# Norm of x in halves of the tokens, the first half scaled by a diagonal matrix in its transpose

## The chip, the cores and the metric

The kernel runs on one core of one Trainium2 chip. The metric is the device time of one execution in microseconds (us), smaller is better. Before the change three runs gave 636.5 us in the median, 636.15 at the lowest and 637.94 at the highest.

## The reference

One decoder layer for 512 tokens of width 1024, in float32:

```
h = RMSNorm(x); proj = h @ w_in            # 8 column groups of attention, RWKV-7 and memory queries
x = x + concat(diff_attention, rwkv7, memory_attention) @ w_out
x = x + hierarchical_moe(RMSNorm(x))       # 16 experts, top-2 inside one of 4 groups
```

Only the first two steps matter here: `h = x * rsqrt(mean(x*x) + eps) * gain`, row by row, and the first projection, whose 256 columns are the inputs of RWKV's small low-rank branches ("lor").

## The kernel before

TensorE multiplies with h as the transposed operand, so x (four tiles `f` of 128 tokens by 1024) has to be normed, transposed and split. Each float32 value is kept as a high part (float32r) and the rest (low part); a product is three matmuls: high by high, high by low, low by high. Weights come through `WeightStream`: a 512 KB chunk lands in `raw`, ScalarE writes its high part `whi` (L96), VectorE its low part `wlo` (L97).

The start is staged like this. For each of the four token tiles `row_scale` (L268) squares and sums on VectorE (L272), GpSimd makes the inverse root (L273, L274), ScalarE multiplies the tile by it (L279; the fourth tile on VectorE, L277). Then TensorE transposes the tile's eight 128-column blocks (L301) into eight PSUM banks, bank k holding block k of all 512 tokens. When all four tiles are in, `split_cols` takes each bank of 512 columns to `hm_h` (ScalarE, L283) and `hm_l` (VectorE, L284). `cols_unit` (L349) is the first projection unit: for each k, for two 128-column groups j, three matmuls of 512 columns (L243, L244, L245, reached through `mm3`), 48 in all, into two PSUM banks; each chunk of weights covers four k. After it ScalarE and VectorE write `lor`, and the next units (k, r, v) follow on TensorE without a break.

Every engine runs its own queue in order. The order within a queue comes from a scheduler that estimates times and follows priorities; the start had no hand-written order. Tiles are reused when their last reader is done, and a reader of a PSUM tile waits for all matmuls into that tile that stand ahead of it in the program.

Of the kernel before, what the change touches and what calls it, by code (L numbers as in the profile page):

```python
# [14 lines left out]
AF = mybir.ActivationFunctionType  # L15
# [32 lines left out]
def VEC(t):  # L48
    return t == 3
# [71 lines left out]
class Weave:  # L121
    """Emits the steps of several streams in the order of their estimated times."""

# [27 lines left out]
def hybrid_layer_kernel(ctx, tc, x, mem, positions, cols, w_in, w_kv, w_out, wa2, g2, ffn, wr, br,  # L151
# [44 lines left out]

# [1 line left out]
    A.preload_act_table_set("sigmoid_and_others")  # L198
    xs = [bR("f1", [P, 2, D]), bR("f2", [P, 2, D])]
    xt = [xs[t // 2][:, t % 2, :] for t in range(NT)]  # L200
    for t in range(NT):
        (nc.sync, nc.scalar)[t % 2].dma_start(xt[t], x[t * P:(t + 1) * P, :])
    col = const.tile([P, N_COLS], F32, name="col")
    nc.scalar.dma_start(col, cols)
    ident = const.tile([P, P], F32, name="ident")
# [61 lines left out]

    def row_scale(src, vec=False):  # L268
        ss = wk.tile([P, 1], F32, name="ssx", bufs=4)
        r = wk.tile([P, 1], F32, name="rsx", bufs=4)  # L270
        scr = b4("aw0", [P, D])
        V.tensor_tensor_reduce(scr, src, src, 1.0, 0.0, op0=ALU.mult, op1=ALU.add, accum_out=ss)  # L272
        G.tensor_scalar(r, ss, 1.0 / D, RMS_EPS, op0=ALU.mult, op1=ALU.add)  # L273
        rooted = G.tensor_tensor(r, r, mhalf, op=ALU.pow)  # L274
        if vec:
            for b in range(2):
                V.tensor_scalar(src[:, b * 512:(b + 1) * 512], src[:, b * 512:(b + 1) * 512], r, None, op0=ALU.mult)  # L277
        else:
            A.activation(src, src, AF.Copy, scale=r)  # L279
        return rooted  # L280
# [4 lines left out]

# [1 line left out]
    banks = [pp() for _ in range(4)] + [pt() for _ in range(2)] + [pc() for _ in range(2)]  # L287
    held = [ws.pair.pop() for _ in range(3)]
    ws.pump()
    for t in range(2):  # L290
        nc.sync.dma_start(m_sb[:, t, :], mem[t * P:(t + 1) * P, :])
# [5 lines left out]
    nc.sync.dma_start(posc, positions.rearrange("o (t p) -> p (o t)", p=P))  # L297
    for t in range(NT):
        rooted = row_scale(xt[t], VEC(t))
        for k in range(KC):  # L300
            T.transpose(banks[k][:, t * P:(t + 1) * P], xt[t][:, k * P:(k + 1) * P], ident)  # L301
    for k in range(KC):
        got_h = split_cols(banks[k], col[:, C_AN + k:C_AN + k + 1], h_hi[:, k, :], h_lo[:, k, :])
        if k == KH:
            ws.pair.extend(reversed(held))
            with tc.issue_after(got_h[0].ins), tc.issue_after(got_h[1].ins):
                ws.pump()

# [18 lines left out]

# [1 line left out]
    r_t = bR("r_t", [P, 2, S])  # L329
# [18 lines left out]

    def cols_unit(dst, mc, flag):  # L349
        ps = [pp() for _ in range(2)]  # L350
        for kh in range(2):
# [13 lines left out]
        flags.add(flag)  # L365
        return None
# [91 lines left out]
    def projections():  # L458
        yield from cols_unit(lor, 6, "lor")
        yield from cols_unit(k_t, 2, "k")  # L460
# [17 lines left out]

# [1 line left out]
    lw = b4("prod", [P, 512])  # L480
# [36 lines left out]
    def rwkv():  # L517
# [85 lines left out]

# [1 line left out]
        for ci in range(4):  # L605
# [60 lines left out]

# [1 line left out]
        V.memset(rs[:, 0:1024:33], 1.0)  # L668
# [91 lines left out]

# [1 line left out]
        y_sb = bR("r_t", [P, NT, 256])  # L762
# [38 lines left out]

# [1 line left out]
    lp = const.tile([P, 2], F32, name="lp")  # L803
# [173 lines left out]

# [1 line left out]
    def out_part(ps, t, i, w, ks, k0, k1, lead=0):  # L979
# [28 lines left out]

# [1 line left out]
    late = ctx.enter_context(tc.tile_pool(name="late", bufs=1, reuse_waits="tile"))  # L1010
# [181 lines left out]

# [1 line left out]
    gslot = rc.tile([P, NE], F32, name="gslot")  # L1194
# [153 lines left out]

# [1 line left out]
    pk = pl(32)  # L1350
# [74 lines left out]
```

## Time and profile before

| | us |
|---|---|
| median of 3 runs | 636.5 |
| span of the profiled execution | 635.0 |
| around that span, in the median run (636.5 less 635.0) | 1.5 |
| TensorE (PE) busy in the span | 605.9 |
| first transpose on PE | 9.72 |
| PE's last long wait of the start ends | 19.49 |

No time of its own is listed for the profiled execution beyond its span. PE, ACT, DVE, POOL and SP are TensorE, ScalarE, VectorE, GpSimd and SyncE; PEld is TensorE's weight load. In a timeline row the first number is the start in us from the start of the span, the second how long the row's instructions took together, `x4` how many there are, and the bracket how long the engine sat idle before it and what released it. Matmuls overlap, so what one costs is read from the distance of starts, not from its own length.

### The profile page before, as it was taken

The page shows a single profiled execution, that of the slowest core. Times are in us where ns is not written, and L with a number is a line of the kernel's source. Part 1 is how long each engine was busy: PE and PEld are TensorE (multiplying, and loading weights), DVE is VectorE, ACT ScalarE, POOL GpSimd, SP SyncE. Part 2 cuts the span into 40 slices and gives each one's busy share as a digit, 9 for nine tenths or more (in the row PEclk, how much of TensorE's full clock was granted, in tenths as well). Part 3 has the DMA queues.
Part 4 walks back from the last instruction along what each step waited for, and adds up shares of the span by engine and source line. Part 5 has one row for each costly group of instructions (what it writes and reads, how often), then busy time and mean ns, then how long its engine had stood idle before and what let it go on. Part 6 is the DMA issues. An engine that isn't in the chain of part 4 may idle for free.

```text
span 635.0 us, 10856 instructions
## 1 busy us (share of the span) xinstructions
PE 605.9 (95%) x3970; PEld 486.2 (77%) x3970; DVE 500.9 (79%) x893; ACT 413.0 (65%) x622; POOL 124.1 (20%) x129
## 2 busy tenths in 40 slices
PE   3899999999999998999999999999999999999992
PEld 3777899999998887769997677777776777777771
DVE  5754988699846698646468999999999999988991
ACT  3667433544457774655246778888888888888880
POOL 6701010344400123304001011110011111320001
PEclk9999999999999999999999999999999999999997
DMA  8523244222332033659698999999999999799913
GB/s 304 167 67 101 66 128 122 78 91 67 102 83 69 1 134 123 243 176 354 237 338 284 358 341 366 382 356 357 362 356 359 361 371 370 251 369 375 336 26 54
DMA packets 77501, 144.17 MB, mean 227 GB/s; under 512 B 12832, under 2 KB 30496, under 8 KB 77440
## 3 DMA queue, kind: packets, MB, share of 16 engines
q1 hardware_dynamic: 69200, 126.07, 56.1%
q0 software_dynamic: 3760, 13.24, 8.9%
q10 hardware_dynamic: 4480, 4.09, 2.0%
q8 instruction: 33, 0.54, 0.3%
q14 instruction: 28, 0.23, 0.1%
HBM read 131.72 MB, written 11.67 MB: 226 GB/s over the span
## 4 chain that ended last, share of the span: by engine, by line
PE 90%; DVE 4%; ACT 2%; DMA 2%; POOL 1%; issue 1%; POOLq 0%; ACTq 0%
PE pp L243 17%; PE pp L245 17%; PE pp L244 17%; PE py L244 4%; PE py L245 4%; PE py L243 4%; PE pp L985 3%; PE pp L986 2%; PE pp L987 2%; PE pp L1267 1%; PE pt L909 1%; PE pc L609 1%; PE py L1123 1%; PE pt L934 1%; PE pl L1090 1%; PE pp L1289 1%
## 5 line engine op out<-in xcount | busy, mean ns | idle before, releaser
L245 PE MATMUL pp<-whi,xl 128*96 128x512 f32 x264 | 104.0, 395 | 0.0
L244 PE MATMUL pp<-wlo,xh 128*96 128x512 f32 x264 | 103.8, 394 | 0.0
L243 PE MATMUL pp<-whi,xh 128*96 128x512 f32 x264 | 101.2, 394 | 0.8 <-ACT xh L1254 0.8
L97 DVE TENSOR_TENSOR wlo<-raw,whi 128x1024 fp32r<-128x1024 f32 x42 | 52.0, 1244 | 19.9 <-ACT whi L96 16.1
L1315 POOL DMA_INDIRECT out<-ye,sidx x16 | 23.2, 1452 | 226.1 <-DVE gidx L1217 105.8
L96 ACT ACTIVATE whi<-raw 128x1024 fp32r<-128x1024 f32 x42 | 44.1, 1058 | 33.0 <-PE pp L245 17.9
L243 PE MATMUL pp<-whi,hm_h 128*128 128x256 f32 x224 | 63.7, 285 | 0.0
L245 PE MATMUL pp<-whi,hm_l 128*128 128x256 f32 x224 | 62.8, 280 | 0.0
L244 PE MATMUL pp<-wlo,hm_h 128*128 128x256 f32 x224 | 62.7, 280 | 0.0
L243 PEld LDWEIGHTS pp<-whi,xh 128*96 128x96 f32 x264 | 42.5, 161 | 19.6 <-ACT xh L1254 1.3
L245 PEld LDWEIGHTS pp<-whi,xl 128*96 128x96 f32 x264 | 42.6, 161 | 18.4
L244 PEld LDWEIGHTS pp<-wlo,xh 128*96 128x96 f32 x264 | 42.5, 161 | 18.2
L244 PE MATMUL py<-wlo,hh 128*96 128x512 f32 x120 | 47.9, 399 | 0.0
L245 PE MATMUL py<-whi,hl 128*96 128x512 f32 x120 | 47.1, 392 | 0.0
L243 PE MATMUL py<-whi,hh 128*96 128x512 f32 x120 | 47.0, 392 | 0.0
L97 DVE TENSOR_TENSOR wlo<-u,whi 128x1024 fp32r<-128x1024 f32 x34 | 41.3, 1238 | 6.6 <-ACT whi L96 6.5
L97 DVE TENSOR_TENSOR wlo<-lraw,whi 128x1024 fp32r<-128x1024 f32 x36 | 42.6, 1217 | 2.8 <-ACT whi L96 2.7
L243 PEld LDWEIGHTS pp<-whi,hm_h 128*128 128x128 f32 x224 | 42.1, 188 | 1.5 <-issue 1.1
L244 PEld LDWEIGHTS pp<-wlo,hm_h 128*128 128x128 f32 x224 | 42.1, 188 | 0.9 <-issue 0.5
L245 PEld LDWEIGHTS pp<-whi,hm_l 128*128 128x128 f32 x224 | 42.1, 188 | 0.3
L96 ACT ACTIVATE whi<-lraw 128x1024 fp32r<-128x1024 f32 x36 | 37.1, 1058 | 5.1 <-PE pp L245 3.6
L96 ACT ACTIVATE whi<-u 128x1024 fp32r<-128x1024 f32 x34 | 35.1, 1055 | 4.6 <-PE pp L245 2.2
(397 smaller groups left out, 1555.3 us busy)
## 6 DMA issues: line engine op xcount, KB each, us to landing
raw<-in_w_in SPq DMA_DIRECT2D x22, 512.0 KB, 3.6
u<-in_wd SPq DMA_DIRECT2D x12, 512.0 KB, 8.0
lraw<-in_wg SPq DMA_DIRECT2D x12, 512.0 KB, 11.3
lraw<-in_wu SPq DMA_DIRECT2D x12, 512.0 KB, 8.7
lraw<-in_wd SPq DMA_DIRECT2D x12, 512.0 KB, 12.4
f<-in_wg SPq DMA_DIRECT2D x11, 512.0 KB, 7.2
u<-in_wu SPq DMA_DIRECT2D x11, 512.0 KB, 12.0
eraw<-in_wd SPq DMA_DIRECT2D x10, 512.0 KB, 13.5
```

Source lines behind the costliest of these rows:

```text
L96: nc.scalar.activation(hi, slot, AF.Copy)
L97: nc.vector.tensor_sub(lo, slot, hi.bitcast(F32))
L243: T.matmul(ps, ah, bh, start=first, stop=False)
L244: T.matmul(ps, ah, bl, start=False, stop=False)
L245: T.matmul(ps, al, bh, start=False, stop=last)
L609: T.matmul(ps[:, h * P:(h + 1) * P], bk[sr(q), ci, h], u1[sr(q), q, ci, h], start=True, stop=True)
L909: T.matmul(po[:, 0:P], aws[i % 2][:, kb * P:(kb + 1) * P], qk["v"][:, kb, h * P:(h + 1) * P], start=kb == 0, stop=kb == qb)
L934: T.matmul(po[rows, :], mv[:, mb, h * 64:(h + 1) * 64], aws[mb][:, 0:512], start=mb == 0, stop=mb == 1)
L985: T.matmul(o, ah, hi[:, k % 4, :], start=k == k0 and i == lead, stop=False, skip_group_check=True)
L986: T.matmul(o, ah, lo[:, k % 4, :], start=False, stop=False, skip_group_check=True)
L987: T.matmul(o, al, hi[:, k % 4, :], start=False, stop=k == k1, skip_group_check=True)
L1315: G.indirect_dma_start(out, bass.IndirectOffsetOnAxis(ap=si, axis=0), ye, None, compute_op=ALU.add)
```

## The change

The four tiles are taken as two halves of 256 tokens. In the first half the tiles are not scaled: `diag[t]` is the identity times the inverse roots, and a true float32 matmul of the tile with `diag[t]` transposes and scales at once (L314 of the new file). The squares of tiles 1 and 3 move to ScalarE (L274). The second half is scaled as before, in half tiles on ScalarE and VectorE (L349, L350), and transposed with the identity (L316). Splits are 256 columns wide (L284, L285) and two blocks k share one bank. The first projection unit is written out in the same place as 96 matmuls of 256 columns (`half_products`, L329 to L331) into the same two banks. ScalarE, VectorE and TensorE get the order of this block as it is written. Tiles 2 and 3 of x are loaded on ScalarE's DMA queue behind `col`.

```diff
-        scr = b4("aw0", [P, D])
-        V.tensor_tensor_reduce(scr, src, src, 1.0, 0.0, op0=ALU.mult, op1=ALU.add, accum_out=ss)
+        if vec:
+            V.tensor_tensor_reduce(b4("aw0", [P, D]), src, src, 1.0, 0.0, op0=ALU.mult, op1=ALU.add, accum_out=ss)
+        else:
+            A.activation(b4("aw1", [P, D]), src, AF.Square, accum_out=ss)
         G.tensor_scalar(r, ss, 1.0 / D, RMS_EPS, op0=ALU.mult, op1=ALU.add)
-        rooted = G.tensor_tensor(r, r, mhalf, op=ALU.pow)
...
+        return r, G.tensor_tensor(r, r, mhalf, op=ALU.pow)
+
+    def row_scale(src):
+        r, rooted = row_root(src)
+        A.activation(src, src, AF.Copy, scale=r)
...
+    def half_turn(hf, k, banks):
+        o = banks[k % 6][:, k // 6 * 256:k // 6 * 256 + 256]
+        for t in range(2):
+            src, dst = xt[2 * hf + t][:, k * P:(k + 1) * P], o[:, t * P:(t + 1) * P]
+            if hf == 0:
+                T.matmul(dst, src, diag[t], start=True, stop=True)
+            else:
+                T.transpose(dst, src, ident)
+
+    def half_split(hf, k, banks):
+        tk = slice(hf * 256, hf * 256 + 256)
+        o = banks[k % 6][:, k // 6 * 256:k // 6 * 256 + 256]
+        return split_cols(o, col[:, C_AN + k:C_AN + k + 1], h_hi[:, k, tk], h_lo[:, k, tk])
+
+    def half_products(hf, ks):
+        tk = slice(hf * 256, hf * 256 + 256)
+        for k in ks:
+            hi, lo = first_w[k // 4]
+            for j in range(2):
+                o, wh, wl = first_ps[j][:, tk], hi[:, k % 4, j * P:(j + 1) * P], lo[:, k % 4, j * P:(j + 1) * P]
+                T.matmul(o, wh, h_hi[:, k, tk], start=hf == 0 and k == 0, stop=False, skip_group_check=True)
+                T.matmul(o, wh, h_lo[:, k, tk], start=False, stop=False, skip_group_check=True)
+                T.matmul(o, wl, h_hi[:, k, tk], start=False, stop=k == KC - 1, skip_group_check=True)
+
+    with tc.manual_schedule(engines={mybir.EngineType.Activation, mybir.EngineType.DVE, mybir.EngineType.PE}):
+        roots = [row_root(xt[0]), row_root(xt[1], False)]
+        for t in range(2):
+            V.tensor_scalar(diag[t], ident, roots[t][0], None, op0=ALU.mult)
+        roots.append(row_root(xt[2]))
+        banks = [pt(), pt(), pc(), pc(), pp(), pp()]
         for k in range(KC):
-            T.transpose(banks[k][:, t * P:(t + 1) * P], xt[t][:, k * P:(k + 1) * P], ident)
-    for k in range(KC):
-        got_h = split_cols(banks[k], col[:, C_AN + k:C_AN + k + 1], h_hi[:, k, :], h_lo[:, k, :])
-        if k == KH:
-            ws.pair.extend(reversed(held))
-            with tc.issue_after(got_h[0].ins), tc.issue_after(got_h[1].ins):
-                ws.pump()
+            half_turn(0, k, banks)
+        weights()
+        for k in range(4):
+            half_split(0, k, banks)
+        weights()
+        roots.append(row_root(xt[3], False))
+        for k in range(4, KC):
+            half_split(0, k, banks)
+        for i in (2, 3):
+            A.activation(xt[i][:, 0:512], xt[i][:, 0:512], AF.Copy, scale=roots[i][0])
+            V.tensor_scalar(xt[i][:, 512:D], xt[i][:, 512:D], roots[i][0], None, op0=ALU.mult)
+        half_products(0, range(4))
+        banks = [pt(), pt(), pc(), pc(), pp(), pp()]
+        for k in range(4):
+            half_turn(1, k, banks)
+        half_products(0, range(4, KC))
+        for k in range(4, KC):
+            half_turn(1, k, banks)
+        for k in range(KC):
+            got_h = half_split(1, k, banks)
+        half_products(1, range(KC))
```

ScalarE's queue at the start, before (f tiles of x, whi high parts of weights, hm_h high parts of h, pp/pt/pc PSUM banks):

```order
L279 ACTIVATE f_96<-f_96,rsx 128x1024 x2
L279 ACTIVATE f_97<-f_97,rsx 128x1024
L96 ACTIVATE whi_80<-raw_79 128x1024
L283 ACTIVATE hm_h<-pp,col 128x512
L96 ACTIVATE whi_83<-raw_82 128x1024
L283 ACTIVATE hm_h<-pp,col 128x512 x3
L283 ACTIVATE hm_h<-pt,col 128x512 x2
L283 ACTIVATE hm_h<-pc,col 128x512 x2
```

Scaling of the tiles comes first there, and the splits are whole banks of 512 columns.

The same queue in the changed kernel (aw takes the squares that nobody reads, ssx their sum):

```order
L274 ACTIVATE aw_146,ssx<-f_96 128x1024
L96 ACTIVATE whi_80<-raw_79 128x1024
L284 ACTIVATE hm_h<-pt,col 128x256 x2
L284 ACTIVATE hm_h<-pc,col 128x256 x2
L96 ACTIVATE whi_83<-raw_82 128x1024
L274 ACTIVATE aw_196,ssx<-f_97 128x1024
L284 ACTIVATE hm_h<-pp,col 128x256 x2
L284 ACTIVATE hm_h<-pt,col 128x256 x2
L349 ACTIVATE f_97<-f_97,rsx 128x512 x2
L284 ACTIVATE hm_h<-pt,col 128x256 x2
L284 ACTIVATE hm_h<-pc,col 128x256 x2
```

The scaling of the tiles stood first and now, for the second half (L349), stands behind the first half's eight splits, two weight chunks and a square.

TensorE's queue before, from its last transposes to the first products:

```order
L301 MATMUL pp<-ident,f_97 128x128 x4
L301 MATMUL pt<-ident,f_97 128x128 x2
L301 MATMUL pc<-ident,f_97 128x128 x2
L243 MATMUL pp<-hm_h,whi_80 128x512
L244 MATMUL pp<-hm_l,whi_80 128x512
L245 MATMUL pp<-hm_h,wlo_81 128x512
```

All 32 transposes stand ahead of the first product there.

TensorE's queue in the changed kernel: the last diagonal products, the first products of the first half, and the place where the second half's transposes begin (qmT is the diagonal matrix):

```order
L314 MATMUL pt<-qmT_132,f_96 128x128
L314 MATMUL pt<-qmT_133,f_96 128x128
L329 MATMUL pp<-hm_h,whi_80 128x256
L330 MATMUL pp<-hm_l,whi_80 128x256
...
L331 MATMUL pp<-hm_h,wlo_81 128x256
L316 MATMUL pt<-ident,f_97 128x128 x4
L316 MATMUL pc<-ident,f_97 128x128 x4
L329 MATMUL pp<-hm_h,whi_83 128x256
```

Transposes of the second half now stand between the products of the first half's blocks 0 to 3 and those of its blocks 4 to 7, and the queue is worked off in this order.

## Rows read from the trace of the kernel before

**Rows 1.** The page's first lines: the span, and each engine's busy time.

```profile
span 635.0 us, 10856 instructions
PE 605.9 (95%) x3970; PEld 486.2 (77%) x3970; DVE 500.9 (79%) x893; ACT 413.0 (65%) x622; POOL 124.1 (20%) x129
```

**Rows 2.** Waits of PE: who for whom, us in total, times, longest.

```profile
PE pp L301 <- ACT f L279: 10.3, 2, 9.7
PE pp L243 <- DVE hm_l L284: 1.6, 2, 0.8
```

**Rows 3.** Timeline of PE, from its first transpose to the second unit.

```profile
9.72 1.11 PE L301 MATMUL pp<-ident,f 128*128 128x128 f32 x4 [9.72 <-ACT f L279]
...
14.07 1.06 PE L301 MATMUL pp<-ident,f 128*128 128x128 f32 x4
...
15.35 0.39 PE L301 MATMUL pc<-ident,f 128*128 128x128 f32 x2
15.57 0.60 PE L301 MATMUL pp<-ident,f 128*128 128x128 f32 x4
...
17.41 0.50 PE L243 MATMUL pp<-hm_h,whi 128*128 128x512 f32 x1 [0.80 <-DVE hm_l L284]
...
20.53 0.39 PE L245 MATMUL pp<-hm_h,wlo 128*128 128x512 f32 x1
...
34.27 0.38 PE L439 MATMUL pt<-ident,kT 128*128 128x128 f32 x2
```

**Rows 4.** Timeline of the start: squares on DVE, inverse roots on POOL.

```profile
5.28 1.23 DVE L272 CUSTOM_DVE_ANT_0 aw<-f 128x1024 f32<-128x1024 f32 x1 [3.66 <-DMA f<-in_x]
...
6.54 1.22 DVE L272 CUSTOM_DVE_ANT_0 aw<-f 128x1024 f32<-128x1024 f32 x1
6.61 1.21 POOL L273 TENSOR_SCALAR rsx<-ssx 128x1 f32<-128x1 f32 x1 [3.76 <-DVE ssx L272]
...
7.90 0.58 POOL L274 TENSOR_TENSOR rsx<-rsx,mhalf 128x1 f32<-128x1 f32 x1
...
11.16 0.19 POOL L273 TENSOR_SCALAR rsx<-ssx 128x1 f32<-128x1 f32 x1
```

**Rows 5.** Timeline of PE: float32 products of 128 columns, then products of 256.

```profile
85.88 1.49 PE L609 MATMUL pc<-u,f 64*128 64x128 f32 x14
87.30 0.39 PE L244 MATMUL pp<-wlo,hm_h 128*128 128x256 f32 x1
87.52 0.28 PE L245 MATMUL pp<-whi,hm_l 128*128 128x256 f32 x1
...
90.93 0.28 PE L245 MATMUL pp<-whi,hm_l 128*128 128x256 f32 x1
```

**Rows 6.** ACT and DVE: timeline rows, and an accumulator read from the groups.

```profile
21.41 2.05 ACT L96 ACTIVATE whi<-raw 128x1024 fp32r<-128x1024 f32 x2
34.07 0.63 ACT L524 ACTIVATE ths<-lor 64x512 f32<-64x512 f32 x1
44.54 0.47 ACT L283 ACTIVATE v_da<-pt,col 128x256 fp32r<-128x256 f32 x1
44.91 0.71 ACT L553 ACTIVATE f<-k_t,col 128x512 f32<-128x512 f32 x1
...
46.03 0.48 DVE L284 SCALAR_TENSOR_TENSOR qT<-pt,col,v_da 128x256 fp32r<-128x256 f32 x1 [0.29 <-ACT v_da L283]
...
L858 ACT ACTIVATION_READ_ACCUMULATOR f<-f,mx 128x1 f32 x20 | 3.8, 191 | 0.0
```

**Rows 7.** Timeline of PE at 245 to 251: three waits.

```profile
245.23 0.68 PE L779 MATMUL pc<-f,f 128*64 128x64 f32 x8 [0.80 <-DVE f L775]
...
248.67 0.68 PE L784 MATMUL pc<-f,u 64*64 64x64 f32 x8 [0.44 <-DVE f L781]
...
250.81 0.56 PE L985 MATMUL pp<-whi,hm_h 128*128 128x256 f32 x1 [0.43 <-ACT pown L879]
```

**Rows 8.** Windows of PE: stretch, length, busy (count), granted clock, DMA share, GB/s.

```profile
251.00:254.00 3.00, 3.00 (x15) 0.50 0.83 298
```

More of the change, by code (lines that the diff above doesn't have):

```diff
@@ L200, in hybrid_layer_kernel @@
     xt = [xs[t // 2][:, t % 2, :] for t in range(NT)]
-    for t in range(NT):
-        (nc.sync, nc.scalar)[t % 2].dma_start(xt[t], x[t * P:(t + 1) * P, :])
     col = const.tile([P, N_COLS], F32, name="col")
+    nc.sync.dma_start(xt[0], x[0:P, :])
+    nc.scalar.dma_start(xt[1], x[P:2 * P, :])
     nc.scalar.dma_start(col, cols)
@@ L266, in hybrid_layer_kernel, with row_root @@
     m_lo = bR("qT", [P, KC, M], F32R)
-    def row_scale(src, vec=False):
+    def row_root(src, vec=True):
         ss = wk.tile([P, 1], F32, name="ssx", bufs=4)
         r = wk.tile([P, 1], F32, name="rsx", bufs=4)
-        scr = b4("aw0", [P, D])
-        V.tensor_tensor_reduce(scr, src, src, 1.0, 0.0, op0=ALU.mult, op1=ALU.add, accum_out=ss)
+        if vec:
+            V.tensor_tensor_reduce(b4("aw0", [P, D]), src, src, 1.0, 0.0, op0=ALU.mult, op1=ALU.add, accum_out=ss)
+        else:
+            A.activation(b4("aw1", [P, D]), src, AF.Square, accum_out=ss)
         G.tensor_scalar(r, ss, 1.0 / D, RMS_EPS, op0=ALU.mult, op1=ALU.add)
-        rooted = G.tensor_tensor(r, r, mhalf, op=ALU.pow)
[L275 to L279, printed above, removed]
+        return r, G.tensor_tensor(r, r, mhalf, op=ALU.pow)
+    def row_scale(src):
+        r, rooted = row_root(src)
+        A.activation(src, src, AF.Copy, scale=r)
         return rooted
@@ L284, in split_cols @@
         return first, V.scalar_tensor_tensor(lo, ps, g, hi.bitcast(F32), op0=ALU.mult, op1=ALU.subtract)
-    banks = [pp() for _ in range(4)] + [pt() for _ in range(2)] + [pc() for _ in range(2)]
-    held = [ws.pair.pop() for _ in range(3)]
+    held = [ws.pair.pop() for _ in range(4)]
     ws.pump()
+    for t in (2, 3):
+        nc.scalar.dma_start(xt[t], x[t * P:(t + 1) * P, :])
     for t in range(2):
@@ L297, in hybrid_layer_kernel @@
     nc.sync.dma_start(posc, positions.rearrange("o (t p) -> p (o t)", p=P))
-    for t in range(NT):
-        rooted = row_scale(xt[t], VEC(t))
-        for k in range(KC):
-            T.transpose(banks[k][:, t * P:(t + 1) * P], xt[t][:, k * P:(k + 1) * P], ident)
-    for k in range(KC):
-        got_h = split_cols(banks[k], col[:, C_AN + k:C_AN + k + 1], h_hi[:, k, :], h_lo[:, k, :])
-        if k == KH:
-            ws.pair.extend(reversed(held))
-            with tc.issue_after(got_h[0].ins), tc.issue_after(got_h[1].ins):
-                ws.pump()
+    diag = [b4(f"qmT{t}", [P, P]) for t in range(2)]
@@ new lines, in hybrid_layer_kernel, with weights @@
+    first_ps = [pp() for _ in range(2)]
+    first_w = []
+    def weights():
+        ws.pair.append(held.pop())
+        ws.pump()
+        first_w.append(ws.use())
+    def half_turn(hf, k, banks):
[6 more added lines that the diff above has]
+                T.transpose(dst, src, ident)
@@ L309, in later @@
+    rooted = roots[3][1]
+    ws.pair.extend(reversed(held))
+    with tc.issue_after(got_h[0].ins), tc.issue_after(got_h[1].ins):
+        ws.cool()
     def later():
@@ L347, in hybrid_layer_kernel, with cols_unit @@
     mv = b4("mv", [P, 2, 256])
-    def cols_unit(dst, mc, flag):
-        ps = [pp() for _ in range(2)]
-        for kh in range(2):
+    def cols_unit(dst, mc, flag, ps=None):
+        done_ = ps is not None
+        ps = ps or [pp() for _ in range(2)]
+        for kh in range(0 if done_ else 2):
             hi, lo = ws.use()
@@ L458, in projections @@
     def projections():
-        yield from cols_unit(lor, 6, "lor")
+        yield from cols_unit(lor, 6, "lor", first_ps)
         yield from cols_unit(k_t, 2, "k")
```

## The prediction

> **What bounds the kernel now.** I read the page first: PE is busy for 605.9 of 635.0 us, DVE and ACT far less [rows 1]. A kernel like that ends when PE ends, so a change at the start is worth what it does to the moment from which PE runs without a break. Next the waits of PE: the largest by far, 10.3 us, is for ACT's scaling of the x tiles, 9.7 of it before the first transpose [rows 2]. Then PE's timeline of the start [rows 3]. PE begins at 9.72. The transposes start 0.21 us apart at first (six from 14.07 to 15.35) and 0.11 apart from 15.35 on (two by 15.57): PE's clock is at the lower of its two levels (1.2 GHz) until about 5.6 us after its first work, then at the higher (2.4 GHz). The products start at 17.41 and run without a gap from 20.53. From there 60 products of 512 columns start before the row at 34.27, 0.229 us each. The row at 20.53 is the ninth of the first unit's 48, so the remaining 40 end at 20.53 + 40 x 0.229 = 29.7. That moment, the end of the first projection unit on PE, is what I compare; behind it PE goes on in both kernels with the same work.
>
> **The start of PE.** What is removed: ACT's scaling in front of the first transposes, and the wait of the first inverse root behind the second square. Before, the first square began at 5.28 and the second at 6.54 [rows 4], so both tiles had landed by then. POOL's first small step took 1.21 us while DVE squared, but 0.19 at 11.16 with DVE almost idle [rows 4]. Now DVE has nothing to do behind the first square, so I count 0.19 and then 0.58 for the power [rows 4]: the first root at about 7.5. The second tile is squared on ACT from about 5.8: 1.03 us (half of the pair of 2.05) and an accumulator read of 0.19 [rows 6], 7.0; its two POOL steps follow the first root and end at about 8.3. With some 0.3 us for the diagonal on DVE PE runs steadily from 8.65, 1.1 us earlier than before.
>
> **The diagonal products.** They take the place of 16 transposes. A true float32 product of 128 columns goes to PE as two instructions: 14 instructions, seven products, took 85.88 to 87.30, 0.203 us for each product at the higher clock level, against 0.11 for a transpose [rows 5, 3]; so 0.43 at the lower level. All at the lower level they end at 8.65 + 16 x 0.43 = 15.5, all at the higher at 8.65 + 16 x 0.203 = 11.9. Nothing in the rows says when the clock rises here, so I take the 5.6 us of before: at 14.25, after 13 products, and the last three take 0.6, end 14.85. The earlier start is eaten by the doubled price. On this one step the Trainium skill, "TensorE: Matmul & The Clock Gate", section Terms, speaks against the change more strongly: it says the transpose mode is four times faster for float32 than an ordinary pass. The rows show twice. What the four would make of the time is a rival below.
>
> **The queue of ACT.** This is the step I give most weight. A reader of a PSUM tile waits for all matmuls into it that stand ahead, and block 6 shares the bank of block 0, block 7 that of block 1. So the first split can begin only behind the 14th of the 16 products and the second behind the last, at about 14.95; the halves don't overlap with the slow products. From there ACT works off its queue in order: seven more splits of 256 columns at 0.37 (44.54 to 44.91) = 2.6; a weight chunk, 1.03; the square of the fourth tile, 1.03 + 0.19; two half tiles scaled, for which a copy of 512 columns stands, 0.63 each, 1.26 [rows 6]. Sum 6.1: the second half's tiles are scaled at 21.05. PE in the meantime has only the 24 products of blocks 0 to 3. Products of 256 columns start 0.114 apart (30 steps from 87.52 to 90.93 [rows 5]), 2.7 us behind the first low part at 14.5 + 0.47 + 0.48 = 15.45 [rows 6], so it is through at 18.1. Then it stands before the second half's transposes for some 2.9 us, and 24 products whose operands have long been ready stand behind them in the queue. Nothing covers this wait: DVE, POOL and the loads all have slack there, and ACT's queue is what PE waits for.
>
> **The rest of the unit.** From 21.05: 8 transposes at 0.11 = 0.9, 24 products = 2.75, 8 transposes = 0.9, end at 25.6. Again no split of the second half can begin before the last blocks are transposed, so a second, short stop follows: one split on ACT and one on DVE, 0.47 + 0.48 + 0.1 for the hand-overs [rows 6] = 1.05 (before it was much the same: two such stops, 1.6 in sum [rows 2]). From 26.6 the remaining 47 products take 5.35: 31.95. The products themselves cost the same as before, 96 x 0.114 = 10.9 against 48 x 0.229 = 11.0.
>
> **The sum.** 31.95 - 29.7 = +2.3 us. It is made against the execution with the span of 635.0; the median of the runs is 636.5, 1.5 of it outside the span, which the change does not touch: 636.5 + 2.3 = **638.8 us**, 0.36% slower. With the bounds of the diagonal products (11.9 and 15.5) the unit ends between 29.0 and 32.6: -0.7 to +2.9, 635.8 to 639.4. Its own range, if the split pitch or the copies are off by a tenth too: 637.6 to 639.8. What else moves I cost at nothing. The zero fill and masks on POOL come some 6 us later, since POOL's queue waits for the fourth tile's sum; they are wanted by later units. Loads of x tiles 2 and 3 are queued behind a 26 KB load and not behind other x tiles, and are needed at 9 and 17 us. The second unit's weight splits follow the last splits on ACT and DVE and would be there at about 31: if they are late by some tenths, PE waits that long once.
>
> **Rivals.**
> 1. *The clock falls in the new gap.* At 245 to 251 PE waited 0.80, 0.44 and 0.43 us among small matmuls, and behind it the granted clock was 0.50 for the whole of 251 to 254 [rows 7, 8]. So much waiting was enough there, and 2.9 us in one piece is more. Against it: at the start PE also waited, 1.6 us in two pieces among products of 512 columns [rows 2], and kept its 0.229 afterwards. A fall as long as that one, 3.0 us at half the clock, costs up to 1.5, less if part of it lies in the gap: 638.8 + 1.5 = 640.3.
> 2. *The queue of ACT is not the bound, since the clock rises early.* If most of the diagonal products run at the higher level, everything behind them slides forward: 635.8 at best, 637 with half of them. For it: PE's work is denser from the start than before. Against it: the 5.6 us of before, also of dense work but for 0.6 us.
> 3. *Not slower: the middle gives it back.* PE's three waits at 245 to 251 (1.67 in sum) are for a chain of small steps on DVE and ACT, and the fall of the clock behind them costs another 1.5 [rows 7, 8]. If the later products leave this chain relatively earlier and the waits close, 3.2 come back: 638.8 - 3.2 = 635.6. It decides once more than 2.3 are regained. Against it: the chain is fed by the same projection units, which all come later by the same amount, so it moves along with PE.
> 4. *Four times a transpose.* By the section Terms of "TensorE: Matmul & The Clock Gate" in the Trainium skill a diagonal product would cost four transposes. As a mechanism here: 0.86 at the lower level, 0.43 at the higher; 6.5 of them by 14.25, the other 9.5 take 4.1, end at 18.35 in place of 14.85: 638.8 + 3.5 = 642.3. The seven products at 0.203 of [rows 5] are against it, though on 64 of the 128 rows.
>
> **How the numbers follow.** What a measurement of this kernel can tell from no change is about 0.3%, 1.9 us: below 634.6 is faster, above 638.4 slower. Forecast 0.45; the falling clock 0.17; the early clock 0.22; the middle 0.12; four times 0.04. Slower: all of rivals 1 and 4, two thirds of the forecast, a little of rival 2: 0.53. Faster: the far ends of rivals 2 and 3, above all both at once: 0.10. The same: 0.37. The range reaches from just under rival 3, 635.4, to somewhat above rival 1, 641.6.
>
> **What would show it.** Right: PE's first product near 8.6; about 0.43 between the diagonal products; the first split on ACT behind the 14th; a wait of PE for ACT's scaling (L349) of 2 to 3 us, the longest of the start after the first; the second unit's first product near 32. Wrong: the splits starting among the diagonal products, or PE at the second half's transposes without a wait; then the first unit would end before 29.7 and the kernel would be faster. If the unit ends where I say and the total is nevertheless below 637, the middle gave it back.

## The result: 642.05 us, slower by 0.85%

The changed kernel took 642.05 us in the median of four runs (640.33 to 644.51), the kernel before 636.33 beside it: a ratio of 1.0085, interval [1.0061, 1.0109]. Forecast were 638.8 us and slower, at most 641.6; the direction held, the size did not: +5.7 us in place of +2.3. The profiled execution took 640.39 us, the second shortest of the four (the others 640.33, 643.71 and 644.51), so its trace shows about 4 of the 5.7. The first lines of the page after, to be read against [rows 1]:

```profile
span 638.6 us, 11008 instructions
PE 609.1 (95%) x4034; PEld 489.9 (77%) x4034; DVE 501.0 (78%) x899; ACT 414.6 (65%) x633; POOL 122.5 (19%) x129
```

PE is busy 3.2 us longer and the span is 3.6 longer. The waits of PE, of the whole run, answer to [rows 2]:

```profile
PE pt L314 <- DVE qmT L336: 8.2, 2, 8.0
PE pt L316 <- ACT f L349: 2.0, 2, 1.7
PE pt L471 <- ACT aw L454: 1.7, 1, 1.7
```

In order: for DVE's diagonal in front of the first product, for ACT's scaling in front of the second half's transposes, and one in the middle that is put down to a square on ACT. The first two are of the start, and forecast. The third is new, stands at 162 us, and was not. PE's timeline of the start answers to [rows 3] (columns as there):

```profile
8.99 1.65 PE L314 MATMUL pt<-qmT,f 128*128 128x128 f32 x6 [0.22 <-DVE qmT L336]
10.44 1.91 PE L314 MATMUL pc<-qmT,f 128*128 128x128 f32 x8
12.14 1.11 PE L314 MATMUL pp<-qmT,f 128*128 128x128 f32 x8
13.09 1.06 PE L314 MATMUL pt<-qmT,f 128*128 128x128 f32 x8
14.27 0.38 PE L329 MATMUL pp<-hm_h,whi 128*128 128x256 f32 x1
...
17.48 0.28 PE L331 MATMUL pp<-hm_h,wlo 128*128 128x256 f32 x1
19.50 0.33 PE L316 MATMUL pt<-ident,f 128*128 128x128 f32 x1 [1.74 <-ACT f L349]
20.11 0.55 PE L316 MATMUL pt<-ident,f 128*128 128x128 f32 x3 [0.28 <-ACT f L349]
20.50 0.60 PE L316 MATMUL pc<-ident,f 128*128 128x128 f32 x4
20.85 0.36 PE L329 MATMUL pp<-hm_h,whi 128*128 128x256 f32 x1
...
31.21 0.39 PE L243 MATMUL pp<-hm_h,whi 128*128 128x512 f32 x1
```

The diagonal products come in pairs of instructions. Eight instructions take 1.70 us from 10.44 to 12.14 and 0.95 from 12.14 to 13.09, so a product costs 0.43 at the lower level of the clock and 0.24 at the higher, which begins at 12.26, so that the first of the second eight still ran ahead of it. In the first experiment below, where the rise comes at 11.44, eight of them take 0.90, 0.23 a product:

```profile
11.78 1.06 PE L314 MATMUL pp<-qmT,f 128*128 128x128 f32 x8
12.68 1.06 PE L314 MATMUL pt<-qmT,f 128*128 128x128 f32 x8
```

Then follow the 24 products of blocks 0 to 3, the forecast wait for ACT, and the second unit's first product at 31.21. In the kernel before that product stands at 29.68:

```profile
29.68 0.39 PE L243 MATMUL pp<-hm_h,whi 128*128 128x512 f32 x1
```

So the start costs **1.5 us** between these two traces. It varies with the execution: the same start of before has this product at 30.19 and 30.21 in the traces of experiments 10 and 2, where the clock rises at 16.1 and 17.4 in place of 15.35. ACT's queue over the same time:

```profile
13.74 0.92 ACT L284 ACTIVATE hm_h<-pt,col 128x256 fp32r<-128x256 f32 x2 [2.89 <-PE pt L314]
14.56 0.83 ACT L284 ACTIVATE hm_h<-pc,col 128x256 fp32r<-128x256 f32 x2
15.28 1.07 ACT L96 ACTIVATE whi<-raw 128x1024 fp32r<-128x1024 f32 x1
16.23 1.06 ACT L274 ACTIVATE aw<-f 128x1024 f32<-128x1024 f32 x1
17.18 0.20 ACT L274 ACTIVATION_READ_ACCUMULATOR aw<-f 128x1 f32 x1
17.27 0.84 ACT L284 ACTIVATE hm_h<-pp,col 128x256 fp32r<-128x256 f32 x2
17.98 0.86 ACT L284 ACTIVATE hm_h<-pt,col 128x256 fp32r<-128x256 f32 x2
18.70 1.36 ACT L349 ACTIVATE f<-f,rsx 128x512 f32<-128x512 f32 x2
```

ACT works without a gap from the first split, which began behind the 14th product, to the second scaling at 20.06: the chain that the forecast named. It is 6.3 us long with the first split in it, and 5.9 from the second split on, where the forecast counts 6.1.

So most of the loss lies behind the start. To find it I paired every PE instruction of the two traces by source line and position and followed the distance of their starts. One landmark of it is a group of eight small matmuls near the end of the RWKV chain, in before and after:

```profile
241.65 0.68 PE L784 MATMUL pc<-f,u 64*64 64x64 f32 x8
```

```profile
247.27 0.68 PE L842 MATMUL pc<-f,u 64*64 64x64 f32 x8
```

The lag grew from 1.5 us at the end of the first unit to 5.6 there. Behind it it shrinks once, to 4.0: the half-speed stretch at 251 to 254 [rows 8] is absent from this trace of the changed kernel, which gives back 1.65. From 255 us to the end the lag is constant within 0.15 (3.93 at the last product). The same landmarks in all runs (behind a name the number of its experiment below), with the differences from before in brackets. The start, the group and the last product are read from one traced execution of each kernel; the last column is the median of all its executions. Experiments 1 to 4, 5 to 8, 9 to 11 and 12 ran on four chips, each beside the kernel before, so between them the ratios compare, and the medians only roughly.

| run | second unit starts | RWKV group | last product | half speed from | median us |
|---|---|---|---|---|---|
| before | 29.68 | 241.65 | 622.77 | 250.9 | 636.3 to 637.3 |
| after | 31.21 (+1.5) | 247.27 (+5.6) | 626.70 (+3.9) | none | 642.05 |
| after again (4) | 33.67 (+4.0) | 251.25 (+9.6) | 630.76 (+8.0) | 20.7, 208.5 | 642.95 |
| old order (1) | 30.89 (+1.2) | 244.52 (+2.9) | 625.51 (+2.7) | 253.8 | 639.19 |
| new order, old start (2) | 30.21 (+0.5) | 248.07 (+6.4) | 627.56 (+4.8) | 164.2 | 639.58 |
| stream times (3) | 31.74 (+2.1) | 246.01 (+4.4) | 627.03 (+4.3) | 255.4 | 640.87 |
| old PE order (5) | 31.23 (+1.6) | 244.72 (+3.1) | 625.77 (+3.0) | 254.2 | 639.91 |
| fill gap (6) | 30.56 (+0.9) | 244.37 (+2.7) | 623.72 (+1.0) | none | 637.21 |
| no diagonal (7) | 31.66 (+2.0) | 245.13 (+3.5) | 624.61 (+1.8) | 20.0 | 639.68 |
| both (8) | 28.47 (-1.2) | 242.50 (+0.9) | 623.47 (+0.7) | 252.3 | 636.38 |
| no POOL subtractions (9) | 30.95 (+1.3) | 242.93 (+1.3) | 622.35 (-0.4) | none | 637.38 |
| the same, before (10) | 30.19 (+0.5) | 242.16 (+0.5) | 623.18 (+0.4) | 251.7 | 635.25 |
| both, free order (11) | 28.61 (-1.1) | another place | 623.70 (+0.9) | none | 637.89 |
| both, subtractions on DVE (12) | 28.07 (-1.6) | 241.43 (-0.2) | 620.98 (-1.8) | none | 634.75 |

Each stretch at half speed lasted 3.4 us. The one at the very end, which all traces have, and which goes on behind the last product, is left out of the table. In the eleventh run the group stands in another place of PE's order, so it is no landmark there. Three of the twelve executions of experiment 2 took 657.9 to 659.0 us at a granted clock of 0.962; its 639.58 is the median of the other nine.

### The profile page after: what moved, and what is told of

Its sections match the earlier page's. It is cut to its first block, busy times and chain, and to the rows that moved or that the text cites. A ratio compares the mean times of both kernels' runs of the same rounds, so it can differ in the third digit from the quotient of the medians.

```text
span 638.6 us, 11008 instructions
## 1 busy us (share of the span) xinstructions
PE 609.1 (95%) x4034; PEld 489.9 (77%) x4034; DVE 501.0 (78%) x899; ACT 414.6 (65%) x633; POOL 122.5 (19%) x129
## 4 chain that ended last, share of the span: by engine, by line
PE 91%; ACT 3%; DVE 2%; DMA 2%; issue 1%; POOL 0%; POOLq 0%; ACTq 0%
PE pp L243 17%; PE pp L245 16%; PE pp L244 16%; PE py L244 4%; PE py L245 4%; PE py L243 4%; PE pp L1043 2%; PE pp L1044 2%; PE pp L1045 2%; PE pt L967 2%; PE pp L1325 1%; PE pc L667 1%; PE py L1181 1%; PE pt L992 1%; PE pl L1148 1%; PE pp L1347 1%
## 5 line engine op out<-in xcount | busy, mean ns | idle before, releaser
L97 DVE TENSOR_TENSOR wlo<-raw,whi 128x1024 fp32r<-128x1024 f32 x42 | 51.8, 1246 | 14.1 <-ACT whi L96 13.7
L97 DVE TENSOR_TENSOR wlo<-u,whi 128x1024 fp32r<-128x1024 f32 x34 | 41.3, 1240 | 6.6 <-ACT whi L96 6.5
L97 DVE TENSOR_TENSOR wlo<-lraw,whi 128x1024 fp32r<-128x1024 f32 x36 | 42.6, 1218 | 2.8 <-ACT whi L96 2.8
```

Of the source, the lines that this page charges most:

```text
L97: nc.vector.tensor_sub(lo, slot, hi.bitcast(F32))
```

## The experiments

The theories: (A) the scheduler chose another order behind the start, and this loses some 4 us; (B) the later start alone makes the lag, whatever the order; (C) it is only the stretches at half speed falling elsewhere. In all experiments "old order" means that the instructions behind the start are chained, engine by engine, in the order of the kernel before; nothing waits for data that it did not wait for, and no work is added. In each of these kernels, and in the eleventh, the four stream steps of the third experiment are put back too. A row of `ORDERS` holds the names of one engine's instructions in the old order:

```diff
+    by = {z.name: z for z in nc.cur_bb.bb.instructions}
+    for row in ORDERS:
...
+        for a, b in zip(names, names[1:]):
+            tc.add_manual_dep(by[b], a, mybir.DependencyInfo(mybir.DependencyClass.NoSync, mybir.DependencyReason.DATA))
```

**1. Changed start, old order.**

> The changed kernel's start, line for line, and behind it the instructions of all five engines held in the order that they have in the kernel before (by order-only dependences; nothing waits for anything new, no work is added). Theory A (the start costs about 1.5 us, and the other 4 us come from another order of the instructions behind it, which the scheduler chose anew): 637.0 to 639.0 us, a ratio to the kernel before of 1.001 to 1.004, and on PE no wait near 162 us for L471's operand that the kernel before does not have. Theory B (the lag in the middle follows from the start alone: streams that are 1.5 us later collide with loads and buffers whatever the order): 640.5 to 643, ratio 1.007 to 1.010. Theory C (the clock's phase: the difference is that dips of the granted clock fall elsewhere): the instructions lag by 1.5 us up to the first dip and the total scatters between 636 and 643 with the number of dips.

Measured: 639.19 us, ratio 1.003 [1.0013, 1.0047], against 1.009 [1.0063, 1.0118] for the changed kernel on the same chip. The loss falls from 6.1 to 2.3 us: the order is most of it. The wait near 162 us is gone; PE waits for the same kind of operand 0.5 us at 149 and 0.7 at 174. But with these two the lag still grows by 1.6 us, which no theory had; the ninth run is about that.

**2. Old start, new order on PE.**

```diff
-                if k % 2:
+                if k % 2 and flag != "lor":
                     yield 2.6
```

and PE's instructions behind the start chained in the order of the changed kernel.

> The converse: the kernel before with its own start (norm, transposes, splits and first unit as before), and PE's instructions behind the first unit held in the order that they have in the changed kernel; the other engines' order is left to the scheduler, which then comes out nearly as in the changed kernel. Theory A (order): the middle's loss without the start's, 638.5 to 641 us, ratio 1.003 to 1.007, with the wait of the transposes for ACT's square near 160 us. Theory B (the start alone): 636 to 637, ratio 0.999 to 1.001. Theory C (clock's phase): no offset before the first dip of the clock.

Measured: 639.58 us, ratio 1.0042 [1.0026, 1.0058]: slower without any of the changed start (the diff above takes the stream steps out, as the change did). The lag is 0.5 us at the second unit and 6.4 at the landmark; a half-speed stretch at 164.2 is in it, 1.65 at the price of the one at 251, which leaves 4.2 us to the order, as in the changed kernel (5.6 - 1.5 = 4.1). The wait comes along (PE's timeline):

```profile
162.90 0.63 PE L413 MATMUL pt<-ident,aw 128*128 128x128 f32 x4 [2.08 <-DVE aw L405]
```

**3. The stream times put back.** The four steps of 2.6 of the first unit, which the change dropped, set how far the streams are emitted against each other:

```diff
+        for _ in range(4 if done_ else 0):
+            yield 2.6
```

> The changed kernel, with the four estimated steps of 2.6 that the first unit used to take in the Weave put back (its products stay in the start), so that the other streams are emitted as late against the projections as in the kernel before. PE then shares 3214 instructions in common order with the kernel before, where the changed kernel shares 2957 and the first experiment 3493 (of 3573). Theory A, with the lost steps as the cause of the new order: most of the middle's 4 us come back, 637.5 to 640, ratio 1.002 to 1.006. Theory A, with the later start as what the scheduler's own clock reacts to: still 640 to 643, ratio 1.006 to 1.010. Theory B: 641 to 643.

Measured: 640.87 us, ratio 1.0052 [1.0037, 1.0066]. From the second unit to the landmark the lag grows by 2.3 us where the changed kernel's grows by 4.1. So the dropped steps are one cause of the loss behind the start, not the whole.

**4. The changed kernel again.**

> The changed kernel once more, beside the others on the same chip. Theories A and B: 640 to 644 us, ratio 1.007 to 1.010, and in the profile the same offsets against the kernel before at 80 us and 250 us (+1.5 to +2, and +4 to +6). Theory C: another profile shows the offsets in other places, as the dips of the clock fall.

Measured: 642.95 us, ratio 1.009 [1.0063, 1.0118]. The offsets of the middle repeat (+5.6 between second unit and landmark, 1.65 of it a half-speed stretch at 208.5), but the start is 2.5 us worse. 0.9 of it lie ahead of the second half's transposes (20.43 against 19.50; the clock rose at 13.90 against 12.26):

```profile
20.43 0.33 PE L316 MATMUL pt<-ident,f 128*128 128x128 f32 x1 [1.74 <-ACT f L349]
```

The other 1.5 lie behind them. Two windows of PE, of the first trace and of this one (columns as in [rows 8]):

```profile
20.80:24.10 3.30, 3.30 (x32) 1.00 0.43 167
```

```profile
20.80:24.10 3.30, 3.06 (x15) 0.50 0.70 267
```

Right behind the wait for ACT the clock fell to its lower level: rival 1, in one of two traces of the same kernel. Theory C is thus right that such stretches scatter the times (640.8 to 646.1 over this run's executions). Whether they make the difference, the mean granted clock of each execution tells: in the traces here it is 0.993 or 0.994 without such a stretch, 0.990 to 0.992 with one and 0.989 with two. Three of the ten executions of the changed kernel have 0.993 or more, with 640.3 to 640.8 us; 18 of the 29 of the kernel before beside this run have it, with 636.5 in the median. Between 0.990 and 0.992 the medians are 642.9 and 638.0. So at equal clock 4 to 5 us remain, and theory C explains the rest at most; by the same sorting the first experiment is left with about 1.2 in both groups.

**5. Old order on PE alone.** The first experiment with the chain on PE only.

> The changed kernel's start, and behind it only PE's instructions held in the order of the kernel before; ACT, DVE, POOL and the loads are ordered by the scheduler. The first experiment held all five (639.2 us, ratio 1.003). If PE's order is what loses the 4 us of the middle: the same as there, ratio 1.001 to 1.005. If the order on ACT or DVE does it (the extra wait near 162 us is for a square on ACT): 640.5 to 643, ratio 1.006 to 1.010, as in the changed kernel.

Measured: 639.91 us, ratio 1.005 [1.0032, 1.0069], which overlaps that of the first experiment; in the trace the lag grows by 1.5 us as there (1.6), at the same two places, and not at all up to 140 us. So holding the other engines adds nothing that shows. That PE's chain does it and not the stream steps, which are in this kernel too, the times don't tell: the third experiment, with the steps alone, has 1.0052 [1.0037, 1.0066]. The traces speak for the chain: with the steps alone the lag, 2.1 at the second unit, has come to 4.3 by 130 us, and here it stays at 1.6. The chain without the steps was not run.

**6 to 8. The start's own parts,** each on top of the first experiment. Six moves one block of code:

```diff
+        half_products(0, range(4, KC))
         banks = [pt(), pt(), pc(), pc(), pp(), pp()]
         for k in range(4):
             half_turn(1, k, banks)
-        half_products(0, range(4, KC))
```

> The first experiment (changed start, old order behind it, 639.2 us) with one edit in the start: the 24 products of blocks 4 to 7 stand ahead of the second half's transposes on PE, not behind the first four of them. If the wait for ACT's scaling (1.74 + 0.28 us) with these products queued behind it is what the start loses: the products run from 17.5 to about 21, the 16 transposes to about 22, the stop for the splits to about 23, and 48 products to 28.4, where the first experiment ends the unit at 30.8: 2.4 us less, 636.2 to 637.5, ratio 0.998 to 1.001. The clock no longer falls in the gap in some of the executions, so the times scatter less. If instead the splits of blocks 4 to 7 hold the products back (ACT is the bound whatever PE's order): at most 0.8 us less, ratio 1.0015 to 1.003.

Measured: 637.21 us, ratio 1.0004 [0.9993, 1.0015], 2.0 us under the first experiment, 1.7 by the ratios. PE has no wait for L349 any more:

```profile
22.15 0.60 PE L316 MATMUL pt<-ident,f 128*128 128x128 f32 x4
...
24.40 0.38 PE L329 MATMUL pp<-hm_h,whi 128*128 128x256 f32 x1 [0.35 <-ACT hm_h L284]
```

The profiled execution itself gained only 0.3 at the second unit: its clock rose at 14.42, in the first experiment at 11.44. Part of the gain is that the clock falls less often: ten of the twelve executions here have a granted clock of 0.993 or more, in the first experiment four of twelve.

Seven takes the diagonal out:

```diff
-            V.tensor_scalar(diag[t], ident, roots[t][0], None, op0=ALU.mult)
+            A.activation(xt[t][:, 0:512], xt[t][:, 0:512], AF.Copy, scale=roots[t][0])
+            V.tensor_scalar(xt[t][:, 512:D], xt[t][:, 512:D], roots[t][0], None, op0=ALU.mult)
...
-            if hf == 0:
-                T.matmul(dst, src, diag[t], start=True, stop=True)
-            else:
-                T.transpose(dst, src, ident)
+            T.transpose(dst, src, ident)
```

> The first experiment with the first half of x scaled by ACT (columns 0 to 511) and DVE (512 to 1023) and then transposed against the identity as the second half is, without diagonal products. If the doubled price of the fp32 products (32 instructions of 0.24 against 16 of 0.21 at the lower clock level) holds up the first split: PE starts steadily some 0.2 us later, at about 9.1, the transposes end at about 12.5 in place of 14, everything behind moves up by about 1.3 us, 637.5 to 638.3, ratio 1.000 to 1.0025. If the clock rises later for the thinner work of PE, or the scalings take ACT's time in front of the splits: no gain or a loss, 639 to 640.5, ratio 1.003 to 1.006.

Measured: 639.68 us, ratio 1.0044 [1.0032, 1.0056]: no gain. Timeline and a window of PE:

```profile
18.37 0.30 PE L312 MATMUL pt<-ident,f 128*128 128x128 f32 x1 [1.75 <-ACT f L346]
```

```profile
20.10:23.30 3.20, 3.20 (x17) 0.50 0.44 178
```

The second half's transposes begin 0.7 us earlier than in the first experiment (19.08), then the clock falls behind the wait, and the gain is gone. How often it falls there the runs don't show; all six executions have a granted clock of 0.991 or less, which in the traces goes with one stretch at least.

> The two edits together (products of blocks 4 to 7 ahead of the second half's transposes, no diagonal products), the old order behind them. If both theories on the start hold, their gains add, since the one acts in front of the first split and the other behind it: 2.4 + 1.3 us under the first experiment, 635 to 636.5, ratio 0.996 to 0.9995, faster than both kernels. If ACT's queue is the bound of the whole start, the second edit moves ACT up and PE follows, but the first one adds under 0.8: 636.5 to 638.

Measured: 636.38 us, ratio 0.9993 [0.9982, 1.0003], which overlaps that of the sixth run, so whether the diagonal costs anything is not settled (the executions at 0.993 or more, eight here and ten there, speak for it: 636.1 against 637.1 in the median); the two edits together bring the changed start level with the kernel before. Its timeline of PE:

```profile
9.71 0.90 PE L312 MATMUL pt<-ident,f 128*128 128x128 f32 x3 [0.73 <-ACT f L332]
...
20.05 0.60 PE L312 MATMUL pt<-ident,f 128*128 128x128 f32 x4
...
22.30 0.39 PE L325 MATMUL pp<-hm_h,whi 128*128 128x256 f32 x1 [0.35 <-ACT hm_h L284]
```

**9 and 10. DVE and POOL meet.** With the old order the lag still grew by 1.6 us. In the first experiment DVE's chain of small products (`prod`, the triangular inverse) falls behind from 123 us on. One product of it beside POOL's subtraction, in the first experiment, then in the kernel before:

```profile
126.39 1.54 POOL L478 TENSOR_TENSOR kl<-qkf,kT 128x512 fp32r<-128x512 f32 x1 [2.20 <-ACT kT L477]
126.72 1.35 DVE L731 TENSOR_TENSOR prod<-r_t,lor 128x112 f32<-128x112 f32 x1
```

```profile
124.91 0.27 DVE L671 TENSOR_TENSOR prod<-r_t,lor 128x112 f32<-128x112 f32 x1
...
125.16 1.28 POOL L418 TENSOR_TENSOR kl<-qkf,kT 128x512 fp32r<-128x512 f32 x1 [2.26 <-ACT kT L417]
```

In the first experiment POOL began 0.33 us ahead of DVE, and the product took 1.35 us and ended with the subtraction (128.07 and 127.93); in the kernel before DVE began 0.25 ahead, and the product took 0.27. The Trainium skill, "SBUF — State Buffer", section Who interferes with whom, says that a DVE instruction with two SBUF inputs contends with a GpSimd instruction that reads SBUF, and that issue order decides which of the two is blocked. The traces agree: here POOL, which began first, holds DVE, and at 137.45 in the first experiment a subtraction that began 0.05 behind a DVE step of two operands (L97, 1.22) took 2.32 in place of 1.28. The first experiment has four products held in this way (1.07 to 1.55 us), the kernel before two (0.9). This reaches PE through DVE's queue: the sum of squares and the multiply of the norm of q and k (L460, L465), whose result PE transposes, stand between the products there. At the first of the two waits:

```profile
144.85 3.04 POOL L462 TENSOR_TENSOR rsq<-rsq,mhalf 128x16 f32<-128x16 f32 x1 [2.03 <-DVE rsq L461]
148.77 0.63 PE L473 MATMUL pt<-ident,aw 128*128 128x128 f32 x4 [0.50 <-DVE aw L465]
```

POOL stood idle for 2.03 us in front of the inverse root between them, so it was DVE that was late, and not POOL's queue. The edit, on both:

```diff
-                    G.tensor_sub(dsts[j][1], full, dsts[j][0].bitcast(F32))
+                    A.activation(dsts[j][1], full, AF.Copy, scale=0.0)
```

> The first experiment (changed start, old order behind it) with POOL's eight subtractions of the low parts of q and k left out: ACT writes zeros in their place, so the low parts are left out of the computation. In the first experiment PE lies 1.23 us behind the kernel before up to 140 us and 2.87 us from 180 us on, and in between DVE's small products of L731 took 1.07 to 1.55 us in the four places where one of POOL's subtractions ran, 0.2 to 0.45 elsewhere. If the meeting of DVE and POOL makes these 1.6 us: no product of L731 above 0.6 us, and the lag does not grow between 140 and 180 us; 636.8 to 638.2, 1.0 to 1.6 us less than the first experiment (639.2). If it is the late load of r_t alone (0.4 us) or DVE's order: the lag grows by more than 1 us all the same, 638.5 to 640.

> The control: the kernel before, its own order held, with the same eight subtractions left out and zeros written by ACT in their place. In the kernel before two products of L671 took 0.9 us beside a subtraction, and PE has no wait there. If the edit by itself gives nothing where PE does not wait for DVE's chain: 636 to 637.5, ratio 0.998 to 1.001; this also shows whether holding an order costs anything. If POOL's subtractions or DVE's chain cost the kernel before something too: below 635.7.

Measured: 637.38 us (ratio 1.001 [0.9995, 1.0025]) and 635.25 (0.9977 [0.9963, 0.9991]). In the trace of the ninth run the product of before takes its old time, and the lag is 1.28 us from the second unit to 245 without growing:

```profile
125.94 0.27 DVE L731 TENSOR_TENSOR prod<-r_t,lor 128x112 f32<-128x112 f32 x1
```

So the meetings are the 1.6 us in the trace. The medians alone would not show it: the control fell by 1.8 us too, its second case, though PE's lag in its trace is a constant 0.5 (the clock's rise at 16.1); what it gained stays open. Against each other the two differ by 2.1 us; their traces put 0.8 of it on the start (1.3 against 0.5 at the second unit). In the control's trace no lag grows under the held order. What seems to begin the meetings in the first experiment is that the load of `r_t` lands later: DVE's chain starts at 121.14 against 119.49, 1.65 us behind where PE is 1.23 behind. The ninth run has the late load too (121.21) and no growing lag, so the load alone costs PE nothing. But the control has it as well, with the old start (120.47, 0.98 behind where PE is 0.5 behind). So it doesn't need the changed start, and may come with the held order; then the 1.6 us would be a price of the experiment and not of the change. The kernel before with its order held and its subtractions kept, which would tell, was not run, and why the load lands later was not tried.

**11 and 12. Two versions of the mended start.**

> The start of the eighth run (products of blocks 4 to 7 ahead of the second half's transposes, no diagonal products, stream times kept), but with the order behind it left to the scheduler, as in the changed kernel; PE then shares 3043 of 3573 instructions in common order with the kernel before. If the free order costs what it did under the changed start (4 us against the held order, of which 2 with the stream times kept): 638 to 641, ratio 1.002 to 1.007. If the scheduler's order is bad only by chance, or only under a late start: 635.5 to 637.5, ratio 0.998 to 1.001.

Measured: 637.89 us, ratio 1.0013 [1.0001, 1.0025]: the eighth run's start with the order left to the scheduler, 1.5 us over it, 1.3 by the ratios, whose intervals just touch. The free order seems to cost here too, less than under the changed start.

Twelve is the eighth run with the subtractions on DVE:

```diff
-                    G.tensor_sub(dsts[j][1], full, dsts[j][0].bitcast(F32))
+                    V.tensor_sub(dsts[j][1], full, dsts[j][0].bitcast(F32))
```

> The eighth run (products of blocks 4 to 7 ahead of the second half's transposes, no diagonal products, old order behind it: 636.4 us, ratio 0.9993) with the eight subtractions of the low parts of q and k on DVE in place of POOL. Nothing is left out. A DVE step of this size took about 0.69 us in the kernel before (128x512, L405), so the eight cost DVE 5.5 us; the four meetings with POOL, which cost DVE's chain (0.87 + 1.08 + 1.09 + 1.10) = 4.1 us in the eighth run, go. If the meetings are the lag that grows by 1.6 us between 140 and 180 us, and the eight steps fall beside the waits of DVE's chain: 634.8 to 635.8, ratio 0.9965 to 0.9985, faster than both kernels. If the eight steps stand in the chain, the lag stays or grows: 636.2 to 638, ratio 0.999 to 1.002.

Measured: 634.75 us, ratio 0.9972 [0.996, 0.9983]: faster than both kernels, and nothing is left out. One of the eight steps in DVE's timeline:

```profile
125.40 0.68 DVE L475 TENSOR_TENSOR kl<-qkf,kT 128x512 fp32r<-128x512 f32 x1
```

It holds DVE for 0.68 us, where each of the four meetings of the eighth run cost 0.9 to 1.1. The lag between 140 and 180 us is halved and not gone: it grows by 0.8, at a wait of 0.53 for the same kind of operand at 171 us, where the eighth run's grows by 1.6. How much of the gain belongs to the subtractions and could be had without this change is open; the control, which had neither their price on POOL nor on DVE, came to 0.9977.

## Why the prediction was right and wrong

- *The start of PE* (8.65): right, 8.99.
- *The diagonal products*: 0.43 and 0.203 were right and nearly right (0.43 and 0.23), and twice a transpose, so rival 4 is out. The clock's rise, fixed at 5.6 us behind PE's first work, was the weak number: it came 4.3 us behind it here (12.26 - 7.99), 3.5 in the first experiment (11.44 - 7.93) and 7.7 in the second (17.42 - 9.72). Hence the last product at about 14.0 and not 14.85.
- *The queue of ACT*: right in place and cause. The wait is 2.0 in place of 2.9, since everything began 0.9 earlier and PE's first products ended at 17.6, not 18.1. The sixth run shows the cause: with the queued products ahead of the wait it is gone.
- *The rest of the unit*: end at 31.2 in place of 31.95; +1.5 us where +2.3 was forecast. How much it is hangs on the clock's rise: in the fourth experiment's trace, where it came at 13.90, the second half's transposes began 0.9 later. The 1.5 us outside the span were the median of three executions less the span of another; in each execution on record it is 1.7 to 1.9. The sum doesn't hang on it.
- *The step that failed* is the one behind the unit: "behind it PE goes on in both kernels with the same work", and "What else moves I cost at nothing". The work is the same, its order is not, and that costs 4.1 us up to the landmark. The changed kernel shares only 2957 of the 3573 PE instructions in common order with the kernel before. I had looked at the order around the start and taken the rest as a shift. That the order and not the later start does it, the first two experiments show from both sides: the old order under the new start takes 3.8 of the 6.1 us away, and the new order under the old start costs 4.2 in its trace. 1.5 from the start and 4.1 from the order are read from one trace, which also gives back 1.65; that they come near the 5.7 of the medians is chance in part.
- *Where the order loses*, shown for one place: the wait at 162 us. PE, DVE and POOL of the changed kernel:

```profile
155.36 1.97 POOL L476 TENSOR_TENSOR kl<-qkf,kT 128x512 fp32r<-128x512 f32 x1 [1.38 <-ACT kT L475]
156.09 1.70 DVE L729 TENSOR_TENSOR prod<-r_t,lor 128x432 f32<-128x432 f32 x1
157.72 1.21 DVE L458 TENSOR_REDUCE ssq<-aw 128x16 f32<-128x1024 f32 x1
...
159.66 3.19 POOL L460 TENSOR_TENSOR rsq<-rsq,mhalf 128x16 f32<-128x16 f32 x1 [2.33 <-DVE rsq L459]
...
162.88 1.29 DVE L463 TENSOR_TENSOR aw<-pp,rsq 128x512 f32<-128x512 f32 x2
163.72 0.63 PE L471 MATMUL pt<-ident,aw 128*128 128x128 f32 x4 [1.69 <-ACT aw L454]
```

  The releaser named is ACT's square, but the operand is multiplied by DVE (162.88; in the second experiment the same wait is put down to it), which needs POOL's inverse root (done at 162.85), which needs DVE's sum (157.72). In the kernel before this sum starts at 149.53 and PE's transposes at 157.88, 8.4 us behind it; in the new order PE stands before them at 162.03, 4.3 behind it. From the sum to the end of the first multiply it is 5.9 us in both, so the new order makes PE wait. The product that POOL's subtraction held for 1.70 us ahead of the sum adds at most 0.5, since the square that the sum reads was done at 157.22:

```profile
156.62 0.60 ACT L454 ACTIVATE aw<-pp 128x512 f32<-128x512 f32 x1 [1.34 <-PE pp L245]
```

  The other 2.4 us of the 4.1 are spread over 80 to 100 and 190 to 230 us in small pieces, and were not taken apart.
- *Rivals.* Number 1 (the clock falls in the gap) happened in one of two traces of the kernel, and cost the 1.5 us that it said: from PE's first transpose of the second half to the second unit that trace takes 13.2 us, the first 11.7. What it reasons from is no rule: PE's three waits at 245 to 251 are there in the first trace of the changed kernel too (0.81, 0.45 and 0.43), and no fall stands behind them. Number 3 named the middle with the wrong sign: it took 4.1, and gave back 1.65 only where the stretch at 251 was missing. No rival had the middle lose.

## What to carry to other kernels

Where a scheduler sets the order, an edit at the start is an edit of every queue behind it: count how much of each engine's order is kept far from the edit, and give "the order behind it gets worse" a price and a chance of its own. When the loss is not in the edited stage, hold the old order under the new code; that separates the two in one run. Hold the kernel before in its own order as a control, with nothing else changed. On an engine that is never idle, put work with ready operands ahead of a wait, not behind it.

## What the runs showed of the hardware that was not expected

- A DVE product of two operands lasted until POOL's running subtraction was done, and 0.1 to 0.5 us longer (0.9 to 1.7 us for what takes 0.2 to 0.6 elsewhere). The same order on every queue is still not the same in time: where one load landed 0.4 us later against PE, four products were held in place of two.
- PE's clock rose between 3.5 and 7.7 us after its first work over the traces of this case, and fell for 3.4 us right behind a wait of 2 us in two of the traces (20.0 and 20.7), which cost 1.5 us each time; behind the same wait it did not fall in five others (the first of the changed kernel, 1, 3, 5 and 9). The windows print 1.00 for the first microseconds too, where the steps (0.43 for a diagonal product) show the lower level: until the first change is recorded, read the level from the steps.
